# A fused adaLN, convolution and RWKV-7 block on one core: the first phase's instruction order on all engines and transfers, traced as tasks

## The chip, the core and the metric

The kernel runs on one core of one Trainium2 chip. A core has a matrix engine (TensorE, PE in the profile; its weight loads are PEld), VectorE (DVE), ScalarE (ACT), GpSimd (POOL) and SyncE (SP), which here issues the DMA transfers. Each engine works through its own list of instructions in order; an instruction that waits for a semaphore holds up all that stand behind it on that engine. The metric is device microseconds of one execution of the whole program. Numbers are float32; products that need float32 accuracy at speed are made from a high and a low part of each operand (type float32r).

## The reference

What is computed, for 2048 tokens of 1024 channels:

```python
def reference(x, c, ...):
    mod = silu(c) @ ada_w + ada_b
    shift, scale, gate = split(mod, 3)
    h = rmsnorm(x, norm_g) * (1 + scale) + shift
    p = h @ w_in                                   # 1024 -> 9344 columns
    c_val, c_gate, c_og, ts, r_og, g_conv, g_rwkv = split(p)
    # branch A: gated depthwise causal convolution of width 31, LayerNorm over channels
    u = depthwise_conv(c_val * sigmoid(c_gate)) + conv_b
    y_conv = (silu(layernorm(u)) * silu(c_og)) @ w_conv_out
    # branch B: RWKV-7, 16 heads of 64
    r, k, v, w_low, a_low = split(ts + mu * (shifted(ts) - ts))
    decay = exp(-exp(-softplus(-(w0 + tanh(w_low) @ w2)) - 0.5))
    a = sigmoid(a0 + a_low @ a2)
    kk = normalised(k * k_k);  k = k * (1 + (a - 1) * k_a)
    for t: state = state * decay_t - (state kk_t) (kk_t a_t)^T + v_t k_t^T;  o_t = state r_t
    y_rwkv = ((groupnorm(o) + sum(r k r_k) v) * silu(r_og)) @ w_rwkv_out
    m = sigmoid(g_conv) * y_conv + sigmoid(g_rwkv) * y_rwkv
    return rmsnorm(x + gate * (m @ w_out), final_g)
```

## The kernel before

**Tiling.** Tokens go in four blocks of 512 (`NB`, `TB`). Activations are held channel-major: 128 channels on the partitions, 512 tokens in a row. A projection tile is 128 output channels x 512 tokens; it takes 8 slices of the 1024 input channels, and each slice three float32r matmuls (high x high, high x low, low x high): 24 matmuls into one PSUM bank (`mm3k`, `mm3`, L172 to L185, with the matmul on L179). Two such banks alternate (`pm`, tag `main`). There are 73 projection tiles in a block.

**First phase.** A block first makes the LoRA tile (`lora_split`, L953) and then runs four slots (`slot`, L1039). A slot has 18 projection tiles: k, r and v for two pairs of heads, two convolution channels tiles (gate and value each), and eight gate tiles. `FILL` sets the order in which the twelve others go between the k, r and v tiles. The first-phase matmuls of a block are 73 x 24 = 1752, and 7008 in all.

Beside the projections run:

- `pair` (L501): decays, normalised keys and the products k by r of one pair of heads, with small matmuls on the PSUM tag `aux`. Its masked products are written on L590 and scaled on L597 into `As`.
- `group` (L645): for the four heads of a slot. It inverts unit triangular matrices: `As` goes to memory in 16 small DMAs (`dA`), comes back as `La`, 31 steps of two GpSimd operations build the inverse `TT` (L671, L673), it goes out as `dT` and comes back into `As` in 16 small DMAs (L684); VectorE transposes (L705), and TensorE makes the off-diagonal part (`lower`, L718, and `upper`, L722). Then comes the recurrence over 8 chunks of 64 tokens. A round of it is a chain of three links: state by KR (L775), VectorE's Xz (L780), As by Xz (L784), VectorE's uv (L795), tk by uv (L800), VectorE's new state S (L804). At the end the group is normalised (L822 to L831), transposed back (L839), gated and stored in `z_d`.
- `taps` (L878): the depthwise convolution, 31 VectorE operations on 512 tokens for each channel tile (L890).
- `lnorm_first` (L905): the LayerNorm of the block before, read back from memory; `xnorm` (L354): the RMSNorm of the next block; `gate_col`, `presplit`: columns and split weights for later.

**What sets the order.** Only TensorE's order is written by hand (`manual_schedule(engines={PE})`, L1084). The side work is a set of generators. `mm3` advances a clock by `US_K` = 0.684 us for each three matmuls (`tick`), and a generator yields a pair (its own TensorE time, a delay after which it goes on) or a condition. For instance, a group waits 35 + 25 us behind its inverse and 2.6, 2.5 and 3.3 us between the links of a round. The other engines and the DMA queue are ordered by the framework's scheduler, which takes `high_priority(HP)` and, for the taps, a low priority (`-LOWP`) into account.

**Buffers.** `hx` is a ring of seven 128 x 512 tiles for the side work (`HXB`), `w` one of six for weights (`WB`), `t2` one of two for evacuations. Weights of the input projection are split into high and low part in block 0, stored, and loaded split in blocks 1 to 3 (`load_w`, L149).

**Second phase.** `rproj` and `cproj` of block 0 run with the last group's recurrence still under way (L1146 to L1149); then the output projection of each block, with the two branch projections of the next.

Of the kernel before, what the change touches and what calls it, by code (L numbers as in the profile page):

```python
# [9 lines left out]
F32 = mybir.dt.float32  # L10
# [8 lines left out]
P = 128  # L19
# [14 lines left out]
W2 = 4  # L34
# [12 lines left out]
US_MM, US_K = 0.228, 0.684  # L47
LOWP = 1500
# [18 lines left out]
def hybrid_block(ctx: ExitStack, tc: tile.TileContext, x, vecs, convk, w2a2, final_g, ada, w_in, w_co, w_ro, w_o, crow, out,  # L67
                 seq=2048, groups=(0, 1, 2, 3), phase2=True, dbg=None):
    nc = tc.nc
    NB = seq // TB  # L70
    dbg = dbg or {}
# [20 lines left out]
    make_identity(nc, ident)  # L92
# [11 lines left out]

    def rsqrt(y, x_, pool, eng, t=None):
        if t is None:
            t = pool.tile(list(x_.shape), F32, name="rs_t", tag="rs_t")
        eng.tensor_scalar(out=y.bitcast(I32), in0=x_.bitcast(I32), scalar1=-0.5, scalar2=float(0x5F3759DF),
                          op0=ALU.mult, op1=ALU.add)
        for _ in range(3):  # L110
            eng.tensor_tensor(out=t, in0=y, in1=y, op=ALU.mult)
            eng.scalar_tensor_tensor(out=t, in0=t, scalar=-0.5, in1=x_, op0=ALU.mult, op1=ALU.mult)
            eng.scalar_tensor_tensor(out=y, in0=t, scalar=1.5, in1=y, op0=ALU.add, op1=ALU.mult)
# [9 lines left out]
    lo_dve = [False]  # L123
# [7 lines left out]
    def presplit(name, n, half):  # L131

        i = f"{n[0]}_{n[1]}" if name == "o" else n
        back = kept.setdefault((name, n), [dp.tile([P, KT, P], F32R, name=f"k{p_}_{name}{i}", tag=f"k{p_}_{name}{i}")
                                           for p_ in "hl"])
        hs = slice(half * 4, half * 4 + 4)
        st, hi, lo = hx("w_st"), hx("w_hi"), hx("w_lo")
        nc.sync.dma_start(st.rearrange("p (k n) -> p k n", k=4), wsrc[name][n][:, hs, :])
        if name == "o":
            gr = hx("w_gr")  # L140
            nc.sync.dma_start(gr[:, :256], grow_d[n[0] * 256:n[0] * 256 + 256].unsqueeze(0).broadcast_to([P, 256]))
            s4 = st.rearrange("p (k n) -> p k n", n=256)
            nc.gpsimd.tensor_tensor(out=s4, in0=s4, in1=gr[:, :256].unsqueeze(1).broadcast_to([P, 2, 256]), op=ALU.mult)
        nc.scalar.copy(hi.bitcast(F32R), st)
        nc.gpsimd.tensor_tensor(out=lo.bitcast(F32R), in0=st, in1=hi, op=ALU.subtract)
        for d_, s_ in zip(back, (hi, lo)):
            nc.sync.dma_start(d_[:, hs, :].bitcast(F32), s_.rearrange("p (k n) -> p k n", k=4))

    def load_w(name, n, hl=None):  # L149
# [11 lines left out]
        with tc.high_priority(HP):  # L161
            nc.scalar.copy(hi, st)  # L162
            lo_eng = nc.vector if lo_dve[0] or (name != "in" and wcount[0] % 4 < W2) else nc.gpsimd
# [17 lines left out]

    def mm3(ps, w, a):
        for k in range(KT):
            mm3k(ps, w, a, k)
            tick(US_K)  # L185
# [34 lines left out]

    now, tasks = [0.0], []

    class Task:

        def __init__(self, gen):
            self.gen, self.at, self.cond, self.done = gen, now[0], None, False
            tasks.append(self)

        def ready(self):
            return self.at <= now[0] and (self.cond is None or self.cond())  # L230

        def step(self):
            try:
                r = next(self.gen)
            except StopIteration:
                self.done = True
                tasks.remove(self)
                return
            if callable(r):
                self.cond = r  # L240
            else:
                self.cond = None
                now[0] += r[0]
                self.at = now[0] + r[1]

    def poll():
        moved = True
        while moved:
            moved = False
            for t in list(tasks):  # L250
                if not t.done and t.ready():
                    t.step()
                    moved = True

    def tick(us):
        now[0] += us
        poll()

    def drain(*ts):
        poll()  # L260
        while not all(t.done for t in ts):
            at = [t.at for t in tasks if t.at > now[0] and (t.cond is None or t.cond())]
            assert at, "no task can go on"
            now[0] = min(at)
            poll()
# [80 lines left out]
    closed = [None]  # L346

    def hx(name):
        return xp.tile([P, TB], F32, name=name, tag="hx")

    def spare(name):
        return closed[0](name) if closed[0] else hx(name)

    def xnorm(b, tts):  # L354
        if not tts:
            return
        held = []
        for tt in tts:
            t0 = b * TB + tt * P
            ss = e2.tile([P, 8], F32, name="ss")  # L360
            xh = []
            for half in range(2):
                xt = hx("xt")
                nc.sync.dma_start(xt, x[t0:t0 + P, half * TB:half * TB + TB])
                xh.append(xt)
            for half in range(2):
                nc.scalar.activation(hx("xsq"), xh[half], AF.Square, accum_out=ss[:, half:half + 1])
            vs, rs = ss[:, 2:3], ss[:, 3:4]
            with tc.high_priority(HP):
                nc.vector.tensor_tensor(out=vs, in0=ss[:, 0:1], in1=ss[:, 1:2], op=ALU.add)  # L370
                nc.vector.tensor_scalar(out=vs, in0=vs, scalar1=1.0 / D, scalar2=RMS_EPS, op0=ALU.mult, op1=ALU.add)
                rsqrt(rs, vs, e2, nc.vector, ss[:, 4:5])
                for kh in range(2):
# [944 lines left out]
```

## Time and profile before

| | |
|---|---|
| median of 3 runs | 3033.8 us (3033.46 to 3036.6) |
| the profiled execution's own time | 3034.01 us |
| its span, first to last instruction | 3032.2 us |
| mean granted TensorE clock | 0.969 |
| projection matmuls of the first phase (L179, 3 x 2304) | 970.6 + 918.6 + 915.4 us busy |
| convolution taps (L890) | 928 x 0.751 us on DVE |
| inverse on POOL (L671, L673) | 179.8 + 191.3 us |

How to read it: the page is one execution on the chip. A line of the groups of instructions gives source line, engine, operation, output and inputs, shapes and count, then the busy time in us and the mean of one in ns, and then the engine's idle time ahead of them with what ended it. Start-up lasts to about 65 us, the first phase to about 2434 us. TensorE matmuls are pipelined, so neighbours overlap and a busy TensorE is not a TensorE at its peak. Idle time of an engine that is not the bottleneck costs nothing by itself.

### The profile page before, as it was taken

How to read it: one execution, taken by the hardware profiler on the slowest of the kernel's cores; microseconds unless marked ns; L12 is line 12 of the kernel's file. 1: busy time of each engine (PE TensorE's matmuls, PEld its weight loads, DVE VectorE, ACT ScalarE, POOL GpSimd, SP SyncE). 2: the span in 40 equal slices, each digit the busy share in tenths (PEclk: the TensorE clock that was granted, in tenths of full speed). 3: DMA queues.
4: the chain of work that ended last, by engine and by line, in shares of the span. 5: the costliest groups of instructions: out<-in, count | busy, mean ns of one | idle time of the engine just before them, and what ended most of it. 6: DMA issues, size and time to landing. Idle time of an engine off the chain costs nothing. (4 is left out here: it accounts for less than half of the span.)

```text
span 3032.2 us, 51026 instructions
## 1 busy us (share of the span) xinstructions
PE 2817.1 (93%) x18640; PEld 2297.6 (76%) x18640; DVE 2072.0 (68%) x4160; ACT 1001.3 (33%) x1936; POOL 1229.8 (41%) x1790
## 2 busy tenths in 40 slices
PE   6889798999799999999999999999999999899998
PEld 5767686777687777777878777778787778788988
DVE  6867777779676778676767777666778755753433
ACT  4424343434233324242423242323323323421211
POOL 3464637352536355425373655253644500400000
PEclk9989899999899999999999999999999999999999
DMA  8677657686757666857676668565656666976665
GB/s 309 234 247 249 217 204 257 204 268 197 241 187 258 198 203 218 284 173 240 191 257 203 210 217 305 168 208 171 193 184 213 237 210 195 336 250 222 215 222 174
DMA packets 363146, 680.00 MB, mean 224 GB/s; under 512 B 135632, under 2 KB 154384, under 8 KB 362896
## 3 DMA queue, kind: packets, MB, share of 16 engines
q1 hardware_dynamic: 362896, 676.75, 67.0%
q8 instruction: 147, 2.41, 0.3%
q14 instruction: 103, 0.84, 0.1%
HBM read 494.08 MB, written 181.41 MB: 223 GB/s over the span
## 5 line engine op out<-in xcount | busy, mean ns | idle before, releaser
L179 PE MATMUL ps_main<-h_hi,w_hi 128*128 128x512 f32 x2304 | 970.6, 421 | 19.7 <-DMA w_hi<-kh_in 15.1
L179 PE MATMUL ps_main<-h_hi,w_lo 128*128 128x512 f32 x2304 | 918.6, 399 | 7.2 <-POOL w_lo L164 4.0
L179 PE MATMUL ps_main<-h_lo,w_hi 128*128 128x512 f32 x2304 | 915.4, 397 | 1.3 <-DVE h_lo L397 1.1
L890 DVE SCALAR_TENSOR_TENSOR acc<-u,ck,acc 128x512 f32<-128x512 f32 x928 | 696.7, 751 | 15.9
L179 PEld LDWEIGHTS ps_main<-h_hi,w_hi 128*128 128x128 f32 x2304 | 442.9, 192 | 115.5 <-issue 9.9
L179 PEld LDWEIGHTS ps_main<-h_hi,w_lo 128*128 128x128 f32 x2304 | 440.7, 191 | 114.4 <-POOL w_lo L164 6.2
L179 PEld LDWEIGHTS ps_main<-h_lo,w_hi 128*128 128x128 f32 x2304 | 443.6, 193 | 81.6 <-DVE h_lo L397 2.9
L804 DVE SCALAR_TENSOR_TENSOR S<-xo,pe,Se 64x64 f32<-64x64 f32 x512 | 144.5, 282 | 140.1 <-PE xo L800 130.5
L671 POOL TENSOR_TENSOR itmp<-La,TT 128x126 f32<-128x126 f32 (+22 forms) x496 | 179.8, 363 | 130.2 <-DMA La<-dA 85.2
L162 ACT CAST w_hi<-w_st 128x1024 fp32r<-128x1024 f32 x103 | 108.1, 1049 | 301.4 <-DMA w_st<-w_co_t 124.8
L673 POOL TENSOR_TENSOR TT<-TT,itmp 128x126 f32<-128x126 f32 (+22 forms) x496 | 191.3, 386 | 36.8
L164 POOL TENSOR_TENSOR w_lo<-w_st,w_hi 128x1024 fp32r<-128x1024 f32 x50 | 120.4, 2408 | 131.2 <-ACT w_hi L162 67.3
L779 ACT ACTIVATE Se<-S,pe 128x128 f32<-128x128 f32 x256 | 88.9, 394 | 169.5 <-DVE S L804 169.4
L164 DVE TENSOR_TENSOR w_lo<-w_st,w_hi 128x1024 fp32r<-128x1024 f32 x53 | 65.6, 1238 | 97.2 <-PE ps_main L179 54.8
L795 DVE TENSOR_TENSOR uv<-xo,rn 64x256 f32<-64x256 f32 x128 | 53.6, 419 | 111.4 <-PE xo L784 99.3
L784 PEld LDWEIGHTS xo<-Xz,As 128*64 128x64 f32 x1024 | 70.0, 138 | 68.8 <-DVE Xz L780 32.0
L753 ACT COPY Xz<-xo 64x256 f32<-64x256 f32 x128 | 47.0, 367 | 211.9 <-PE xo L758 141.7
L780 DVE TENSOR_TENSOR Xz<-xo,Xz 64x256 f32<-64x256 f32 x128 | 53.5, 418 | 86.0 <-PE xo L775 78.9
L845 POOL TENSOR_TENSOR oc<-oc,zt 128x512 f32<-128x512 f32 x64 | 81.7, 1285 | 66.6 <-ACT oc L841 39.6
L784 PE MATMUL xo<-Xz,As 128*64 128x64 f32 x1024 | 87.9, 230 | 20.9 <-DVE Xz L780 20.8
L590 DVE TENSOR_TENSOR As<-aux,maskA 128x512 f32<-128x512 f32 x128 | 83.0, 682 | 30.9 <-PE aux L587 30.4
L587 PE MATMUL aux<-KR,BK 64*128 64x128 f32 x1024 | 82.2, 291 | 17.8 <-DVE As L590 9.3
(299 smaller groups left out, 5493.7 us busy)
## 6 DMA issues: line engine op xcount, KB each, us to landing
w_hi<-kh_in SPq DMA_DIRECT2D x219, 512.0 KB, 4.2
w_lo<-kl_in SPq DMA_DIRECT2D x219, 512.0 KB, 5.3
w_st<-w_in_t SPq DMA_DIRECT2D x73, 512.0 KB, 4.5
kh_in<-w_hi SPq DMA_DIRECT2D x71, 512.0 KB, 2.9
kl_in<-w_lo SPq DMA_DIRECT2D x71, 512.0 KB, 3.6
lny<-y_d SPq DMA_DIRECT2D x72, 256.0 KB, 4.4
w_hi<-kh_ro SPq DMA_DIRECT2D x32, 512.0 KB, 3.9
w_lo<-kl_ro SPq DMA_DIRECT2D x32, 512.0 KB, 5.3
```

The costliest lines, as they stand in the source:

```text
L162: nc.scalar.copy(hi, st)
L164: lo_eng.tensor_tensor(out=lo, in0=st, in1=hi.bitcast(F32), op=ALU.subtract)
L179: nc.tensor.matmul(ps[:, qs], ww[:, k, :], aa[k][:, qs], start=(k == 0 and t == 0 and q == 0), stop=(k == KT - 1 and t == 2 and q == ms - ...
L587: nc.tensor.matmul(pA[hh][:, c // 2, es], BK[hs, cc, es], KR[hs, cc, es], start=(c == 0), stop=(c == 3), skip_group_check=True)
L590: nc.vector.tensor_tensor(out=Asb[:, hh, c4 * 4:c4 * 4 + 4, :].rearrange("p (a e) n -> p a (e n)", e=2), in0=pA[hh], in1=flat(maskA).unsqu ...
L671: nc.gpsimd.tensor_tensor(out=tmp[:, :ni, :nt], in0=La[:, j:j + 1, j + 1:].broadcast_to([P, ni, nt]), in1=TT[:, :ni, j:j + 1].broadcast_to ...
L673: nc.gpsimd.tensor_tensor(out=TT[:, :ni, j + 1:], in0=TT[:, :ni, j + 1:], in1=tmp[:, :ni, :nt], op=ALU.add)
L779: nc.scalar.mul(Se[:, q, :], Sg[:, q, :], R[q]["pe"][:, c:c + 1])
L784: nc.tensor.matmul(b_[pr_, q, hs], As[q][:, hh, c, kcol(e)], Xz[:, e, q, hs], start=(n == 0), stop=(n == 3), skip_group_check=True)
L804: nc.vector.scalar_tensor_tensor(out=Sg[hs, q, hs], in0=b_[hs, 2 + q, hs], scalar=R[q]["pe"][hs, c:c + 1], in1=Se[hs, q, hs], op0=ALU.mult ...
L845: nc.gpsimd.tensor_tensor(out=oc, in0=oc, in1=zt, op=op)
L890: nc.vector.scalar_tensor_tensor(out=acc if i + 1 < HALO else yj, in0=u[:, i:i + TB], scalar=ck[:, j, i:i + 1], in1=acc, op0=ALU.mult, op1 ...
```

## The change

The first phase is now traced by hand for all five engines and for the DMA issues (`manual_schedule()` without a list): the program order on each engine is the order in which the Python code runs. Which step runs next is decided by a clock kept while tracing. Every instruction goes through a wrapper (`Lane`), so that in a profile of the changed kernel all of them carry the wrapper's line.

- `note` keeps, for every engine and for the DMA, the time until which it is busy (`vt`), for every tile when it is written and last used (`ready`, `used`), and for every pool tag the buffers in use. Costs are constants: `RATE`, `DMA_RATE`, `SEM`, `SWITCH`. TensorE's time is `now`.
- A `Task` has a rank. `poll` runs the first task in rank order whose condition has come: pieces of data are ready (`ok`), an engine's backlog is below a number (`idle`), a PSUM bank is free (`bank`), a ring has room (`Ring.room`), or a flag is set (`when`). Groups and evacuations have rank 0, weight loads 1, pairs 2, side work 3, taps 4. `until` moves the clock on when TensorE has nothing that it may do.
- `group`, `pair`, `taps`, `lnorm_first`, `xnorm`, `gate_col`, `presplit`, `lora_split` and the evacuations are rewritten with such conditions in place of delays, and take tiles from rings and give them back. The evacuation of a projection tile is a task of its own (`evac`); `project` waits until that of the tile before the last is done.
- Weights are loaded two or three tiles ahead (`plan`, `Load`). The split of the next block's input is fed into the last projection of a block (`hstep`), where it stood at the start of the next.
- `slot` starts when the group two slots back is normalised. Five fill tiles instead of two (`FIRST`) stand between the pairs, and the last slot has an order of its own (`LAST`).
- `rproj` and `cproj` of block 0 become tasks as well (`early_rows`, `lsteps`), and `W2` now decides on which engine a weight's low part is made.

```diff
-US_MM, US_K = 0.228, 0.684
-LOWP = 1500
+LAST = ("c", "1", "c", "3", "4", "2", "1", "3", "4", "2")
+DMA_RATE = 330e3
+FIRST = 5
+AHEAD = 0.7
+BANKS = {"aux": 2, "late": 1, "xo": 2}
+SEM, SWITCH = 0.1, 0.1
+RATE = {"DVE": (0.16, 1.08e-3), "ACT": (0.20, 0.8e-3), "POOL": (0.12, 2.2e-3)}
...
+    def note(name, op, out, ins):
+        k_ = key(out)
+        t = max([now[0], vt.get(name, 0.0), used.get(k_, 0.0)] + [ready.get(key(a), 0.0) + SEM for a in ins])
...
+        elif name == "SP":
+            vt["SP"] = t + 0.07
+            vt["DMA"] = max(vt["DMA"], t) + size(out) * out.shape[0] * 4 / DMA_RATE
+            end = vt["DMA"] + 1.9
+        else:
+            c0, c1_ = RATE[name]
+            end = vt[name] = t + c0 + c1_ * max([size(out)] + [size(a) for a in ins[:1]])
...
+    def until(pred):
+        poll()
+        while not pred():
+            ws = [w for w in (t.when() for t in tasks) if w is not None and w > now[0]]
+            now[0] = min(ws)
+            poll()
...
     def mm3(ps, w, a):
         for k in range(KT):
+            until(lambda: len(a[1]) > k)
             mm3k(ps, w, a, k)
-            tick(US_K)
+            if khook[0]:
+                khook[0](k)
+            poll()
...
+    def project(a, src):
+        ahead()
+        w = loads.pop(0)
+        ahead()
+        until(lambda: w.here)
+        drain(*evacs[-2:-1])
+        ps = pm.tile([P, TB], F32, name="ps_main", tag="main")
+        mm3(ps, w.hl, a)
+        Task(w.drop(), 1)
+        return ps
...
     def group(G, before):
-        yield lambda: G.tri == 2
+        yield when(lambda: G.tri == 2)
+        yield ok(*As)
...
+        yield ok(La, TT)
         for j in range(31):
+            yield idle("POOL", 0.5)
...
-        lo_dve[0] = True
-        yield 0.0, 35.0
-        lo_dve[0] = False
-        yield 0.0, 25.0
-        yield lambda: G.pairs == 2 and (before is None or before.done)
+                yield idle("SP", 0.1)
+        yield when(lambda: G.pairs == 2 and (before is None or before.chained))
+        yield ok(*As)
...
-            yield 0.6, 2.6
+            yield ok(Xz)
...
-            yield 1.1, 2.5
+            yield ok(uv)
...
-            yield 0.6, 3.3
+            yield ok(Sg)
...
     def taps(b, j, u, before):
...
         for i in range(HALO):
-            if i % 2:
-                yield 0.0, 2.0
+            yield idle("DVE", AHEAD)
...
     def lnorm_first(b):
...
         for j in range(KT):
+            yield hx.room(3, 1)
+            yj, ct, th = yload(j), hx.take("lnc"), hx.take("lnth")
+            nc.sync.dma_start(ct, co_dram[b][j])
+            yield ok(yj, rl)
             nc.gpsimd.tensor_tensor(out=yj, in0=yj, in1=mean, op=ALU.subtract)
+            yield idle("POOL", 0.3)
             nc.gpsimd.tensor_tensor(out=yj, in0=yj, in1=rl, op=ALU.mult)
...
+    def lora_split(ps, out_):
+        yield hx.room(3)
+        lf, ll, lx = hx.take("lora"), hx.take("lora_lo"), hx.take("lora_x")
...
+    def slot(b, g, h, lora, new):
+        until(lambda: not Gs[:-1] or Gs[-2].normed)
+        G = opened(b, g, h, lora)
+        groups_.append(Task(group(G, Gs[-1] if Gs else None), 0))
...
-    with tc.manual_schedule(engines={mybir.EngineType.PE}):
+    with tc.manual_schedule():
...
-        drain(*pairs_, *convs)
+        drain(*pairs_, *convs, *side, *evacs, *groups_[:-1])
```

More of the change, by code (lines that the diff above doesn't have):

```diff
@@ L33 @@
 HP = 3000
-W2 = 4
+W2 = 0.3
 HB = 8
@@ L218, in xload0 @@
         return xs
[L221 to L265, printed above, removed]
     late, early = ExitStack(), ExitStack()
```

782 lines of the change are left out of this document (544 added, 238 removed).

## The prediction

> **What bounds the kernel now.** The page comes first: its span, busy shares and clock row.
>
> ```profile
> span 3032.2 us, 51026 instructions
> ...
> PE 2817.1 (93%) x18640; PEld 2297.6 (76%) x18640; DVE 2072.0 (68%) x4160; ACT 1001.3 (33%) x1936; POOL 1229.8 (41%) x1790
> ...
> PEclk9989899999899999999999999999999999999999
> ...
> PE 16%; DVE 4%; DMA 2%; POOL 1%; issue 1%; SPq 0%; ACT 0%; DVEq 0%; POOLq 0%; ACTq 0%
> ```
>
> TensorE (PE) sets the time, also in the chain of waits (last line), where it has the largest share. The next view is busy time by stage: start-up, first phase, the stretch in which the last recurrence runs beside block 0's output projections, and the rest.
>
> ```profile
> core 0: us, PE busy (x) PEld busy (x) DVE busy (x) ACT busy (x) POOL busy (x), PEclk, DMA share, GB/s
> ...
> 65.00:2434.00 2369.00, 2210.86 (x15004) 1773.56 (x15003) 1739.45 (x3512) 819.02 (x1572) 1160.60 (x1731) 0.97 0.67 221
> 2434.00:2663.00 229.00, 210.94 (x1369) 177.11 (x1368) 138.68 (x244) 76.64 (x150) 48.08 (x32) 0.96 0.73 250
> ```
>
> In the first phase TensorE is idle for 2369 - 2211 = 158 us, and a granted clock of 0.97 costs about 0.03 x 2369 = 71 us. So 229 us is all that a better order can win there. The second stretch holds 18 us more. Where the idle time goes is in the list of TensorE's waits up to 2434 us:
>
> ```profile
> engine line waited for: us in total, times, longest us
> PE late L839 <- POOL uv L831: 23.3, 4, 16.1
> PE xo L784 <- DVE Xz L780: 20.8, 14, 3.8
> ...
> PE ps_main L179 <- DMA w_hi<-kh_in: 15.1, 3, 5.8
> PE late L839 <- ACT oc L841: 13.4, 14, 1.1
> PE aux L587 <- DVE As L590: 9.3, 7, 4.5
> PE late L722 <- DVE Qs L728: 9.1, 8, 1.9
> PE late L718 <- DVE T L705: 7.9, 2, 4.6
> ...
> PE xo L758 <- DVE S L804: 7.5, 3, 4.4
> ...
> PE ps_main L179 <- ACT w_hi L162: 4.3, 1, 4.3
> PE ps_main L179 <- POOL w_lo L164: 4.0, 4, 1.5
> ...
> PE ps_main L179 <- DVE w_lo L164: 2.0, 1, 2.0
> ```
>
> No single wait rules. About a third belongs to transposes and weights that the fixed delays placed too early, and the rest to short handoffs with VectorE (DVE).
>
> **The part of the change that speaks against it: the triangular inverse.** Each of the 16 groups needs one: mask on VectorE (L590, L597), DMA out (dA) and in (La), 62 GpSimd steps (L671, L673), DMA out (dT) and in (As), eight transposes (L705), and then TensorE's `lower` (L718). The last group, and the one before the last block boundary, show how long that takes:
>
> ```profile
> 2381.48 1.61 DVE L597 TENSOR_TENSOR As<-As,rn 64x512 f32<-64x512 f32 x2
> ...
> 2389.26 1.13 SPq L662 DMA_DIRECT2D La<-dA  x2
> ...
> 2423.16 1.34 SPq L677 DMA_DIRECT2D dT<-TT  x2
> ...
> 2426.97 9.19 SPq L684 DMA_DIRECT2D As<-dT  x16
> ...
> 2435.91 1.94 DVE L705 STREAM_TRANSPOSE T<-As 32x128 f32<-32x128 f32 x8
> ...
> 1801.15 3.41 DVE L597 TENSOR_TENSOR As<-As,rn 64x512 f32<-64x512 f32 x2
> ...
> 1872.40 0.30 DVE L705 STREAM_TRANSPOSE T<-As 32x128 f32<-32x128 f32 x1
> ```
>
> From the end of L597 to the last transpose it takes 2437.85 - 2383.09 = 54.8 us in the one and 1872.70 - 1804.56 = 68.1 us in the other; I take the middle, 61.4. What TensorE does meanwhile is mostly projection matmuls, and their pace under this load is in the busy time of that tile:
>
> ```profile
> 2383.00:2456.00 73.00, 59.82 (x234) 44.88 (x234) 3.41 (x5) 4.79 (x8) 0.93 0.79 264
> ```
>
> 73 / 234 = 0.312 us for each, other matmuls and waits included. In the old TensorE order each group has 216 to 279 projection matmuls between its last L587 matmul and its `lower`, so the inverse is covered. In the new order twelve groups have 180 to 321. Four have far fewer: group 8 of 16 has 96, group 12 has 84, group 15 has 108, group 16 has 93. There `lower` stands in TensorE's queue, and everything behind it waits.
>
> The code says why. At the boundary into blocks 2 and 3 the LoRA product's evacuation waits for three `hx` buffers. The layer norm of the block before holds them, and its GpSimd work goes ahead only when GpSimd's backlog is under 0.3 us, behind the inverse (rank 0, backlog under 0.5 us). The third product may not be traced until that evacuation is done, so the inverse's remaining GpSimd steps, its DMAs and `lower` all land before it. Group 15 meets the rule that a slot opens only when the group two before it is normalised; group 16 meets the `drain` at the end of the phase.
>
> Price of a place: 61.4 us less its matmuls at 0.312. That is 31.5, 35.2, 27.7 and 32.4 us, in sum 126.8. At group 15 another 3.67 rounds of the recurrence stand with no projection between them. What VectorE does in a round is in the groups of instructions:
>
> ```profile
> L890 DVE SCALAR_TENSOR_TENSOR acc<-u,ck,acc 128x512 f32<-128x512 f32 x928 | 696.7, 751 | 15.9
> ...
> L804 DVE SCALAR_TENSOR_TENSOR S<-xo,pe,Se 64x64 f32<-64x64 f32 x512 | 144.5, 282 | 140.1 <-PE xo L800 130.5
> ...
> L795 DVE TENSOR_TENSOR uv<-xo,rn 64x256 f32<-64x256 f32 x128 | 53.6, 419 | 111.4 <-PE xo L784 99.3 <-PE xo L749 10.8
> L780 DVE TENSOR_TENSOR Xz<-xo,Xz 64x256 f32<-64x256 f32 x128 | 53.5, 418 | 86.0 <-PE xo L775 78.9 <-ACT uv L625 5.8
> ```
>
> 0.418 + 0.419 + 4 x 0.282 = 1.97 us, and with one convolution tap in front of each link, as the new order has it, 3 x 0.751 more: 3.67 x 4.2 = 15 us (7 without taps). **Sum: +142 us**; from 4 x 54.8 - 118.9 + 7 = 107 to 4 x 68.1 - 118.9 + 15 = 169, where 118.9 is the 381 matmuls at 0.312.
>
> **What it removes.** The transposes that waited for ScalarE's oc (13.4 here, 5.2 in smaller rows) now wait in the tracing for a free bank, and products go between. Weight waits (15.1 + 4.3 + 4.0 and 3.1 in smaller rows) go, since loads are traced as soon as a ring has room and the next block's split is fed into the last product. Half of the 23.3 us behind uv goes: two of the new slot starts still have that transpose right behind GpSimd work. Together 18.6 + 26.5 + 11.6 = 57 us. Their share of the clock loss is 57 / 158 x 71 = 26 us; four long stalls bring some of it back:
>
> ```profile
> 336.10:353.20 17.10, 4.39 (x14) 3.51 (x15) 9.96 (x22) 4.92 (x7) 7.59 (x7) 0.50 0.64 223
> ...
> 162.00:165.40 3.40, 3.40 (x10) 2.61 (x9) 2.48 (x4) 1.03 (x1) 2.85 (x8) 0.50 0.90 328
> ```
>
> After the 16.1 us gap, 4.39 us of matmuls ran at half clock and lost 2.2 us, so four stalls cost 9. **Sum: -57 - 26 + 9 = -74 us**; bounds: nothing to the whole 229.
>
> By the Trainium skill (TensorE: Matmul & The Clock Gate, "HAM oscillation — how this bites in real kernels") only idle gaps over about 3.4 us cost clock, which would leave most of the 26 us unwon and the sum some 15 us higher. Here the trace disagrees: the second row is at half clock and follows the wait of 2.0 us for w_lo, the last in the list of waits above.
>
> **What it moves without a sure sign.** In the recurrence a round had 33 to 39 projection matmuls between its links, and now has mostly 15 (3, 6, 6). Three are 0.77 us of TensorE's busy time (59.82 / 234 each), in which VectorE must do L780 (0.418), leaving 0.35 us for two handoffs and for a tap that is under way (0.751). A short wait at each of the 384 links costs, at 0.3 us, up to 115 us; the 28 us of L780 and L804 in the list of waits can go at best. I take no change. The clock of the new tracing is too fast in places. It charges 0.71 us for any 512-wide VectorE operation, 0.23 us for a scan of 64, and 0.07 us for a DMA issue:
>
> ```profile
> L524 DVE TENSOR_TENSOR_SCAN M<-one,M 128x64 f32<-128x64 f32 x256 | 90.9, 420 | 8.4 <-ACT M L516 8.1
> ...
> L572 DVE SCALAR_TENSOR_TENSOR rk<-r,hrk,ta 128x512 f32<-128x512 f32 x32 | 43.3, 1352 | 0.3
> ...
> L705 DVE STREAM_TRANSPOSE T<-As 32x128 f32<-32x128 f32 x128 | 31.0, 277 | 9.5 <-DMA As<-dT 8.2
> ...
> L684 SPq DMA_DIRECT2D As<-dT x256: 302/430/1596, 189.1 to 2435.7; - x128
> ```
>
> VectorE has slack over the phase (1739 of 2369 us), so this shows as lateness, not as load. Sixteen small DMAs take 6.9 us against 1.1 modelled, twice a group, so La and As land 11.6 us later than the order assumes. GpSimd's first step and VectorE's transposes then wait at the head of their queues, with weight splits, evacuations and the links of the recurrence behind them. Two PSUM banks cover two products, 48 matmuls or 15 us at the pace above, so I charge nothing to the twelve ordinary groups; without that cover it is up to 12 x 11.6 = 139 us. Choosing VectorE or GpSimd for a weight's low part (W2) and the evacuations as tasks lie beside TensorE's work and are charged nothing; uncovered they would wait on the same banks.
>
> **After the phase.** The last recurrence ends after 111 projection matmuls of the second phase, not 381, so its norm and transposes leave the end of the 229 us stretch. Of the 18 us idle there I take 12 off, bounds 0 and 18.
>
> **Sum.** 142 - 74 - 12 = +56 us. The profiled execution took 3034.0 us by its own time (span 3032.2), the median of the runs is 3033.8: **3090 us**.
>
> **Rivals.**
> 1. *Readiness pays more than four stalls cost.* The new order breaks even when it wins 142 - 12 = 130 of the 229 us. For it: most waits are handoffs that a readiness test is made for, and the idle clock follows them. Against: the links get tighter, and its constants are low for the operations above. If three quarters go (-172), the stalls stay near 120 and 15 come off behind the phase: -67, **2967 us**.
> 2. *Late semaphores.* The head-of-queue waits for La and As are not covered by the PSUM banks: 8 us in each of twelve groups is 96 on top of +56, **3186 us**. It decides as soon as As lands after its transposes' turn; against it, today's transposes (L705 above) wait 8.2 us in all for that DMA.
> 3. *The order hardly matters*, because TensorE is full and stalls trade places: within 0.2% (6 us, about what runs of this kernel can tell apart), **3034 us**.
>
> **How the numbers follow.** The forecast has 0.42 with its own range 3045 to 3135, rival 1 0.36, rival 2 0.17, rival 3 0.05. Rival 1 lies some 55 us either side of its figure, rival 2 about as far, so 2955 to 3190 leaves out a little under 2 in 10. Faster 0.37, same 0.06, slower 0.57.
>
> **What would show it.** Right: four TensorE gaps of 20 us or more, at `lower` or right ahead of it, near 51%, 76%, 94% and 100% of the first phase's projection matmuls, with GpSimd in its inverse steps or SP issuing As; the waits for oc and for weights nearly gone; short waits at L780's consumer more frequent. Wrong: no such gaps, or a granted clock of 0.99 in the phase. If VectorE's idle time behind As is large in every group, rival 2 was right.

## The result and the profile after

| | before | after |
|---|---|---|
| median of the runs beside each other, us | 3033.6 (3029.5 to 3036.6, 4 runs) | 3251.0 (3250.0 to 3252.3, 4 runs) |
| ratio after / before | | 1.072, 95% interval 1.0704 to 1.0735 |
| span of the profiled execution, us | 3032.2 | 3249.3 |

The changed kernel is 217 us slower. The prediction had the sign, with 56 us. These are the lines of the page of the changed kernel that answer to those of before (span, busy shares, granted clock in 40 slices, chain of waits by engine), and the mean granted clock:

```profile
span 3249.3 us, 51086 instructions
...
PE 2869.5 (88%) x18640; PEld 2324.2 (72%) x18640; DVE 2153.6 (66%) x4153; ACT 997.1 (31%) x1936; POOL 1270.6 (39%) x1797
...
PEclk9999999999899999799989997999998969999999
...
PE 27%; DVE 7%; POOL 6%; DMA 5%; issue 2%; SPq 2%; ACT 1%; DVEq 0%; POOLq 0%; ACTq 0%
```

```profile
core 0: 3249.3 us, clock 0.938
```

The 217 us split in two. TensorE's idle time went from 3032.2 - 2817.1 = 215.1 to 3249.3 - 2869.5 = 379.8 us: +165. Its busy time went up by 52.4 us with the same 18640 matmuls; they ran slower, and the mean granted clock fell from 0.969 to 0.938. The clock records of the two traces account for nearly all of it: TensorE was busy at half clock for 141 us before and for 243 us after, and half of the difference is 51 us. Where the idle time is, the list of TensorE's waits of the changed kernel says (us in total, times, longest):

```profile
PE late L126 <- DVE T L126: 134.3, 13, 34.8
PE ps_main L126 <- ACT h_hi L126: 18.8, 3, 8.5
PE ps_main L126 <- ACT w_hi L126: 18.3, 5, 5.6
PE late L126 <- POOL uv L126: 18.0, 5, 7.3
...
PE aux L126 <- POOL KR L126: 16.4, 13, 3.2
PE ps_main L126 <- DMA w_hi<-kh_in: 16.1, 5, 4.7
PE aux L126 <- ACT wl L126: 13.0, 5, 6.0
PE xo L126 <- DVE Xz L126: 10.8, 18, 1.8
...
PE ps_main L126 <- POOL w_lo L126: 8.9, 5, 3.2
...
PE xo L126 <- DVE S L126: 3.6, 5, 1.1
...
PE late L126 <- ACT oc L126: 1.7, 2, 0.9
```

The first line is `lower` behind VectorE's transposes: 134.3 us, where before it was 7.9 us on the PSUM tag `late` and 2.9 on `aux`, so +123.5. Four waits make up 108.7 of it, in groups 8, 12, 15 and 16 (first matmul of `lower`, the idle time ahead of it in brackets):

```profile
1340.31 0.23 PE L126 MATMUL late<-T,As 32*32 32x32 f32 x1 [31.78 <-DVE T L126]
...
1988.33 0.23 PE L126 MATMUL late<-T,As 32*32 32x32 f32 x1 [34.77 <-DVE T L126]
...
2431.19 0.26 PE L126 MATMUL late<-T,As 32*32 32x32 f32 x1 [12.31 <-DVE T L126]
...
2626.55 0.26 PE L126 MATMUL late<-T,As 32*32 32x32 f32 x1 [29.86 <-DVE T L126]
```

All other idle time is +41 us, of which 31 lie in the first phase, for which the prediction had -57. The waits for oc are nearly gone, those for weights are not, and waits for h_hi and wl are new. Two stretches of the changed kernel's timeline show where new ones arise (start, duration, queue, instruction):

```profile
644.41 8.37 SPq L126 DMA_DIRECT2D dA<-As  x16
...
657.24 0.43 SPq L126 DMA_DIRECT2D hf<-xT  x1
...
663.59 0.80 PE L126 MATMUL ps_main<-h_hi,w_hi 128*128 128x512 f32 x1 [8.51 <-ACT h_hi L126]
...
885.62 9.85 SPq L126 DMA_DIRECT2D As<-dT  x16
...
895.52 0.43 SPq L126 DMA_DIRECT2D wf<-w2a  x1
...
898.08 0.79 PE L126 MATMUL aux<-lw,wl 128*128 128x512 f32 x1 [5.95 <-ACT wl L126]
```

The issues of the inverse's sixteen small DMAs occupy SP for 8.37 and 9.85 us. One of them takes 0.43 us in the median, 6.9 us for sixteen; most of the rest is SP's own waits between them. The traced clock charges 0.07 for one, 1.1 us for sixteen. The load of the next block's input (hf) and of the decay weights (wf), a few places further back on SP, come that much later, and with them a cast on ScalarE and a product. Last, the busy time by stage, cut at the last projection of the first phase and at the first output product (the second is how long block 0's two products and the last recurrence take), before and then after:

```profile
65.00:2435.00 2370.00, 2211.86 (x15009) 1774.22 (x15007) 1739.45 (x3512) 819.35 (x1573) 1160.60 (x1731) 0.97 0.67 221
2435.00:2556.00 121.00, 113.59 (x766) 90.91 (x766) 64.04 (x122) 33.28 (x63) 5.02 (x4) 0.96 0.59 195
```

```profile
65.00:2597.00 2532.00, 2248.99 (x15012) 1792.56 (x15012) 1823.09 (x3519) 815.89 (x1571) 1179.05 (x1705) 0.94 0.62 206
2597.00:2780.00 183.00, 131.64 (x782) 100.65 (x782) 92.26 (x150) 51.13 (x94) 64.29 (x66) 0.80 0.53 182
```

The phase takes 162 us more, the stretch behind it 62 more (29.9 of them the stall of group 16); the rest of the second phase gives 7 back.

### The profile page after: what moved, and what is told of

The parts are those of the page before. It is cut to its first block, busy times and chain, and to the rows that moved or that the text cites. A ratio compares the mean times of both kernels' runs of the same rounds, so it can differ in the third digit from the quotient of the medians.

```text
span 3249.3 us, 51086 instructions
## 1 busy us (share of the span) xinstructions
PE 2869.5 (88%) x18640; PEld 2324.2 (72%) x18640; DVE 2153.6 (66%) x4153; ACT 997.1 (31%) x1936; POOL 1270.6 (39%) x1797
## 4 chain that ended last, share of the span: by engine, by line
PE 27%; DVE 7%; POOL 6%; DMA 5%; issue 2%; SPq 2%; ACT 1%; DVEq 0%; POOLq 0%; ACTq 0%
PE ps_main L126 17%; PE pout L126 5%; PE xo L126 4%; SPq L126 2%; POOL TT L126 1%; POOL itmp L126 1%; DVE acc L126 1%; PE aux L126 1%; DVE S L126 1%; PE late L126 1%; POOL lny L126 1%; DMA out<-xt 1%; DVE y L126 0%; DMA w_lo<-kl_in 0%; DMA dA<-As 0%
## 5 line engine op out<-in xcount | busy, mean ns | idle before, releaser
L126 PE MATMUL ps_main<-h_hi,w_hi 128*128 128x512 f32 x2304 | 986.6, 428 | 60.0 <-ACT h_hi L126 18.8
L126 PE MATMUL ps_main<-h_hi,w_lo 128*128 128x512 f32 x2304 | 929.5, 403 | 12.3 <-POOL w_lo L126 6.6
L126 POOL TENSOR_TENSOR w_lo<-w_st,w_hi 128x1024 fp32r<-128x1024 f32 (+1 forms) x89 | 181.2, 2035 | 317.1 <-ACT w_hi L126 283.5
L126 POOL TENSOR_TENSOR itmp<-La,TT 128x126 f32<-128x126 f32 (+22 forms) x496 | 195.7, 395 | 145.5 <-DMA La<-dA 114.5
L126 ACT CAST w_hi<-w_st 128x1024 fp32r<-128x1024 f32 (+1 forms) x135 | 127.3, 943 | 251.8 <-DMA w_st<-w_co_t 126.6
L126 ACT ACTIVATE th<-ps_main 128x512 f32<-128x512 f32 x160 | 95.4, 596 | 319.2 <-PE ps_main L126 272.9
L126 POOL TENSOR_TENSOR lny<-lny 128x512 f32<-128x512 f32 x90 | 117.6, 1313 | 125.4 <-DMA lny<-y_d 116.2
L126 PE MATMUL xo<-uv,As 128*64 128x64 f32 x2048 | 156.9, 230 | 1.5 <-issue 0.9
L126 PEld LDWEIGHTS xo<-uv,As 128*64 128x64 f32 x2048 | 135.2, 141 | 14.2 <-DVE S L126 6.9
L126 PE MATMUL late<-T,As 32*32 32x32 f32 x512 | 25.6, 215 | 134.3 <-DVE T L126 134.3
L126 PEld LDWEIGHTS late<-T,As 32*32 32x32 f32 x512 | 23.4, 131 | 141.1 <-DVE T L126 72.4
```

The source lines that it names most:

```text
L126: r = f(*a, **k)
```

## The experiments

Each is the changed kernel (3251.0 us) with the edit shown, timed beside the kernel before (medians 3030.5 to 3034.9 us in the four groups of runs).

| run | us | ratio to before, 95% interval |
|---|---|---|
| 1 the wait at four `lower` taken away | 3236.9 | 1.0658 (1.0633 to 1.0684) |
| 2 layer norm's step at 0.7 us of backlog | 3202.1 | 1.0551 (1.0530 to 1.0572) |
| 3 traced order on TensorE alone | 3376.2 | 1.1125 (1.1106 to 1.1145) |
| 4 an SP issue charged 0.45 us | 3151.7 | 1.0382 (1.0363 to 1.0400) |
| 5 last group's `lower` held back | 3236.6 | 1.0670 (1.0652 to 1.0689) |
| 6 six constants | 3014.7 | 0.9932 (0.9908 to 0.9955) |
| 7 six constants, other values | 2998.1 | 0.9884 (0.9869 to 0.9900) |
| 8 as 7, SP issue at 0.07 | 3077.3 | 1.0149 (1.0125 to 1.0173) |
| 9 as 7, second pair after 5 fills | 3062.5 | 1.0082 (1.0057 to 1.0108) |
| 10 as 7, queues free after the phase | 2985.4 | 0.9843 (0.9813 to 0.9873) |
| 11 second pair after 2 fills | 3254.5 | 1.0741 (1.0717 to 1.0765) |
| 12 as 11, SP issue at 0.45 | 3213.7 | 1.0607 (1.0580 to 1.0634) |

### 1. Is a stall the wait of `lower` for the inverse?

```diff
+    CUT = (7, 11, 14, 15)
...
-            ENT[TRE].tensor_tensor(out=tri, in0=tri, in1=rq[sl].rearrange("p c h -> p h c").unsqueeze(3).broadcast_to(
+            ENT[TRE].tensor_tensor(out=tri, in0=tri, in1=(zer if CUT is None or 4 * b + G.g in CUT else rq)[sl].rearrange("p c h -> p h c").unsqueeze(3).broadcast_to(
...
-                        nc.sync.dma_start(As[q][sl, hh, e::2, sl], dT[:, q, hh, :, e, bk, :])
+                        if CUT is None or 4 * b + g in CUT:
+                            tc.nc.sync.dma_start(spill[sl, hh], dT[:, q, hh, :, e, bk, :])
+                            note("SP", "dma_start", As[q][sl, hh, e::2, sl], [dT])
+                        else:
+                            nc.sync.dma_start(As[q][sl, hh, e::2, sl], dT[:, q, hh, :, e, bk, :])
```

> The changed kernel with every instruction in its place, but in groups 8, 12, 15 and 16 the sixteen transfers of the inverse land in a spare tile and not in As, and the triangle of As is multiplied by zeros (the output is wrong there). So `lower` has nothing to wait for in these four groups, while GpSimd, SP and the transfers do all their work. Stall theory (the four waits are their own price): the four TensorE gaps, 31.8 + 34.8 + 12.3 + 29.9 = 109 us, go, and 5 to 15 us of half clock behind them: 3127 to 3137 us, still some 100 over the kernel before. Rival (in a stall the other engines catch up, so that without it their lateness shows elsewhere): half of it returns as other waits, 3180 to 3200 us. Second rival (all of the loss hangs on the stalls): near 3034 us.

Measured: 3236.9 us, 14 less. No theory had so little: most of the four gaps stayed, and in the same places (27.2, 29.1, 10.1 and 22.0 us, 88 of 109). The waits of this run:

```profile
PE late L126 <- DVE T L126: 59.8, 9, 22.0
PE late L126 <- ACT la L126: 56.4, 2, 29.1
```

Its timeline at group 8 shows why:

```profile
1327.49 0.24 POOL L126 TENSOR_TENSOR TT<-TT,itmp 128x16 f32<-128x16 f32 x1
1327.69 1.26 POOL L126 TENSOR_TENSOR lny<-lny,lnr 128x512 f32<-128x512 f32 x1
...
1328.98 0.81 ACT L126 ACTIVATE lnth<-lny,hlb,hlg 128x512 f32<-128x512 f32 x1 [20.77 <-POOL lny L126]
...
1330.67 0.69 DVE L126 SCALAR_TENSOR_TENSOR lny<-lnth,lny 128x512 f32<-128x512 f32 x1 [16.23 <-ACT lny L126]
...
1332.84 1.76 DVE L126 STREAM_TRANSPOSE T<-As 32x128 f32<-32x128 f32 x8
...
1334.74 0.23 PE L126 MATMUL late<-T,As 32*32 32x32 f32 x1 [27.22 <-ACT la L126]
```

The transposes need nothing from the inverse any more. But in VectorE's queue they stand behind a layer norm step, that one waits for ScalarE's, that one for GpSimd's, and GpSimd's stands behind the last step of the inverse. All queues run in traced order, so all of them meet at the point where the traced clock ran ahead without a product for TensorE. (ScalarE's la, which the list names, ended 0.07 us after the last transpose, so that the two waits end together; la stands behind the same layer norm step, by way of lora on VectorE.) Taking away one wait of this knot gave back only the 2 to 8 us by which it was the last.

### 2. The place in the tracing that makes two of the stalls

```diff
             yield ok(yj, rl)
             nc.gpsimd.tensor_tensor(out=yj, in0=yj, in1=mean, op=ALU.subtract)
-            yield idle("POOL", 0.3)
+            yield idle("POOL", 0.7)
             nc.gpsimd.tensor_tensor(out=yj, in0=yj, in1=rl, op=ALU.mult)
```

> One constant: the layer norm's GpSimd step may be traced with GpSimd 0.7 us behind, not 0.3. By the traced order this gives `lower` 222 and 213 projection matmuls of cover in groups 8 and 12 where the changed kernel has 96 and 84, and 120 and 141 in groups 15 and 16 where it has 108 and 93. Stall theory: the gaps of 31.8 and 34.8 us go, 60 matmuls at 0.312 us take 19 us off the other two, and about 5 us of half clock go with them: 3155 to 3165 us. Rival (the layer norm's steps now stand between the inverse's on GpSimd and make it later): one gap of 10 to 20 us stays at each of the two boundaries, 3180 to 3200 us. If hx was not the cause: 3251 us.

Measured: 3202.1 us, 49 less; more time than the stall theory's 3155 to 3165, and just beyond the rival's range, though not by its mechanism:

```profile
PE late L126 <- DVE T L126: 43.2, 11, 10.5
PE aux L126 <- ACT wl L126: 38.6, 9, 7.9
...
PE ps_main L126 <- ACT o_hi L126: 16.7, 2, 16.3
```

The waits at `lower` fell from 134.3 to 43.2 us and none is over 10.5; in groups 8 and 12 they are 2.1 and 2.6 us. So the boundary stalls did come from the layer norm's step; that it acts by holding the `hx` ring is read from the code. But wl rose from 13.0 to 38.6, o_hi from 2.8 to 16.7, and DVE mr from 4.8 to 15.6. We read this as late loads and casts that the stalls had covered; no run separates it. Groups 15 and 16, with 120 and 141 matmuls of cover, waited 10.5 and 5.7 us, where 61.4 us less their matmuls at 0.312 gives 24.0 and 17.4.

### 3. Do the fixed orders of the other four queues cost by themselves?

```diff
-    with tc.manual_schedule():
+    with tc.manual_schedule(engines={mybir.EngineType.PE}):
```

> TensorE keeps the traced order; the orders of VectorE, ScalarE, GpSimd and SP are left to the scheduler, as in the kernel before. Queue theory (the rest of the loss, some 90 us beside the stalls, comes from the other four queues keeping the traced order, in which a small transfer or a cast stands behind sixteen DMA issues): the waits for h_hi (18.8), wl (13.0), w_hi (18.3) and KR (16.4) mostly go, the four gaps at `lower` stay near 109: 3180 to 3200 us. Rival (it is TensorE's order alone): within 10 us of 3251. Second rival (the scheduler's own order does not fit this TensorE order): 3270 us or more.

Measured: 3376.2 us. In time the queue theory and the first rival fall, and the second rival holds. `lower` alone now waits 193.7 us on the tag `late`, the longest 55.9:

```profile
PE late L126 <- DVE T L126: 193.7, 9, 55.9
```

The scheduler's order brings the inverse later than this TensorE order needs it. But one part of the queue theory's forecast did come: the waits for h_hi, wl, wlo, KR and the projections' weights, 34.3 us before the change and 99.2 in the changed kernel, are 22.8 us here (h_hi 4.4, w_hi 7.6, w_lo 10.8, none for the others). So these belong to the traced order of the other four queues, as far as the longer stalls did not cover them.

### 4. The charge for a DMA issue

```diff
-            vt["SP"] = t + 0.07
+            vt["SP"] = t + 0.45
```

> One constant of the traced clock: an issue on SP is charged 0.45 us (the trace shows 0.32 to 0.6), not 0.07. The order changes everywhere: `lower` is short of cover in groups 6, 10, 14 and 16 (81, 114, 102 and 165 matmuls against 197 needed), the other twelve have 201 or more. Stall theory: 36 + 26 + 30 + 10 = 102 us of gaps in place of 124, and no bare recurrence at group 15: 3200 to 3220 us. Queue theory adds that waits behind bursts of issues (h_hi, wl, part of w_hi) fall by 30 to 40 us with their clock: 3160 to 3180 us. If both fail it stays at 3240 us or more.

Measured: 3151.7 us, 99 less, more than either theory gave. Around groups 6, 10 and 14, short of cover, TensorE does stall, but ahead of their `lower`, at the last transposes of groups 5, 9 and 13, for which the next slot waits:

```profile
964.44 0.69 PE L126 MATMUL late<-ident,uv 128*128 128x128 f32 x2 [17.66 <-POOL uv L126]
...
2219.84 0.69 PE L126 MATMUL late<-ident,uv 128*128 128x128 f32 x2 [14.63 <-POOL uv L126]
```

The one between them is 18.96 us; that is 51 us where 36, 26 and 30 were expected. `lower` itself waits 11.7 us on `late`, where the changed kernel has 134.3; this, less what came at uv, is most of the 99 us. The waits that the queue theory named fell little: h_hi 18.8 to 14.7, wl 13.0 to 9.8, w_hi behind ScalarE 18.3 to 13.4 and behind the DMA 16.1 to 10.4, KR 16.4 to 14.4. With wlo and w_lo they are 82.8 us, 16 less, not 30 to 40.

### 5. The last group

```diff
+    closed = [None]
...
-        yield when(lambda: G.pairs == 2 and (before is None or before.chained))
+        yield when(lambda: G.pairs == 2 and (before is None or before.chained) and (
+            4 * b + g < 15 or closed[0] is not None and now[0] >= closed[0] + 15.0))
...
+        closed[0] = now[0]
         early.close()
```

> Only the last group's inverse is followed later: its transposes and `lower` may be traced from 15 us (by the traced clock) after the end of the first phase, so that projection rows of block 0 stand ahead of `lower` (129 matmuls of cover, not 93). If the stall at group 16 is `lower` traced too early, its gap (29.9 us) falls by the 36 matmuls, 11 us, and the recurrence ends later but still beside the second phase: 3235 to 3240 us. Rival (the first rows are not ready either, their loads start only when the phase is closed and their splits stand in the same queues): the gap only changes its name, from VectorE's T to ScalarE's o_hi: 3251 us.

Measured: 3236.6 us, 14 less. The time is in the first range, but that is luck: the trace speaks for the rival. The wait for o_hi is 32.7 us in one piece, and `lower` waits 109.2 in all, 25 less. The first rows of block 0 are as late as the inverse, and the gap changed its name. TensorE's idle time is the same in all (380.0 us, 379.8 in the changed kernel); what fell is its busy time, from 2869.5 to 2858.6 us, with less of it at half clock.

### 6 and 7. The constants of the clock and of the ranks

Run 6 (in run 7 AHEAD is 0.4, the scans' backlog 1.0, and the layer norm of the block before starts in slot 1, not 2):

```diff
-W2 = 0.3
+W2 = 0.0
...
-FIRST = 5
-AHEAD = 0.7
+FIRST = 2
+AHEAD = 0.5
...
-            vt["SP"] = t + 0.07
+            vt["SP"] = t + 0.45
...
-                yield idle("DVE", 0.3)
+                yield idle("DVE", 2.0)
...
-            yield idle("POOL", 0.3)
+            yield idle("POOL", 0.7)
```

> Six constants of the tracing and nothing else: an SP issue charged 0.45 us, the layer norm's GpSimd step allowed 0.7 us of backlog, the scans 2.0 us of VectorE backlog, taps 0.5 us ahead in place of 0.7, the second pair of a group after 2 fills in place of 5, and a low part on VectorE as soon as GpSimd is the later. By the traced order every group has 231 to 318 projection matmuls between its last L587 matmul and `lower`. Clock theory (readiness tracing is sound, its clock and its ranks misplaced the inverse and with it all five queues): no gap over 6 us at `lower` or at the transposes of uv in the phase, half-clock time near that of before (193 us), 3030 to 3070 us. Rival (five queues in a fixed order cost by themselves: waits for weights, wl, h_hi and KR and the clock behind them stay as they are): 3090 to 3120 us.

> As the run before it, but taps 0.4 us ahead, scans 1.0 us, and the layer norm of the block before starts one slot earlier. Same cover (222 to 339 matmuls). Both theories expect it within 10 us of that run; more than 20 us between them would mean that the place of single tasks still decides, not the cover of the inverse.

Measured: 3014.7 and 2998.1 us, both under every range given, and 0.7 and 1.2% faster than the kernel before. The clock theory's signs came nearly as stated: in run 6 the longest wait at `lower` is 6.8 us, and half clock took 198 us. Of the rival's waits those for weights did stay (47.1 us in the changed kernel, 51.1 and 46.4 here), while h_hi and wl went from 31.8 to 8.1 and 4.6. Of run 7, the page, the wait at `lower`, the mean clock and the busy time by stage:

```profile
span 2997.8 us, 51087 instructions
...
PE 2810.1 (94%) x18640; PEld 2288.6 (76%) x18640; DVE 2128.6 (71%) x4158; ACT 998.6 (33%) x1936; POOL 1244.8 (42%) x1792
```

```profile
PE late L126 <- DVE T L126: 16.4, 5, 9.0
```

```profile
core 0: 2997.8 us, clock 0.970
```

```profile
65.00:2363.00 2298.00, 2187.16 (x15011) 1756.43 (x15012) 1788.02 (x3515) 818.66 (x1573) 1168.26 (x1739) 0.98 0.68 227
2363.00:2532.00 169.00, 135.45 (x782) 102.47 (x781) 97.98 (x152) 49.88 (x92) 49.28 (x27) 0.82 0.58 194
```

The phase is 72 us shorter than before the change (2298 against 2370), with 111 us idle where it had 158, and the clock is back. The stretch behind it keeps 48 of the 62 us that the change added. The two runs lie 17 us apart with the same cover, more than the 10 expected and less than the 20 that would have spoken for single places; this stays undecided.

### 8, 9, 11 and 12. One constant at a time

Run 8 sets the SP charge of run 7 back to 0.07, run 9 its FIRST back to 5; run 11 is the changed kernel with FIRST at 2, run 12 the same with the charge of 0.45.

> The second retimed kernel with one constant set back: an SP issue is charged 0.07 us again. The cover of the inverse stays (189 to 285 matmuls in every group). If the charge for SP is what the retiming needs (bursts of sixteen issues stand ahead of loads that the order counts on), waits for weights, wl and h_hi come back by 30 to 60 us and the clock with them: 3050 to 3090 us. If the cover of the inverse alone decides: 2990 to 3015 us.

> The second retimed kernel with one constant set back: the second pair of a group starts after 5 fills again, not 2. Cover falls to 144 and 129 matmuls in groups 14 and 16, to 183 in group 4, and the slots wait longer for the group two before. If the place of the second pair sets when the inverse can start and so what stalls, two gaps of 15 to 20 us and longer waits behind uv come back: 3050 to 3080 us. If not: within 10 us of 2998.

> The changed kernel with one part of the change undone: the second pair of a group follows after 2 fills, as before the change, not after 5. Cover of the inverse by the traced order: group 15 gets 213 matmuls (108), groups 8, 12 and 16 stay short with 102, 78 and 48. By the price of the stalls alone: group 15 gives back 12 us of gap and 9 us of bare recurrence, group 16 costs 14 more: 3240 to 3250 us. If the late second pair costs by itself in every group (64 us in the retimed kernel): 3185 to 3200 us.

> Both at once on the changed kernel: 2 fills, and an SP issue charged 0.45 us. Cover is short in group 8 (99) and group 16 (135) alone. If the two effects add (99 us for the charge, 64 for the second pair): 3085 to 3095 us. If the slots' wait for the group two before, which sets the price of a late second pair, is only reached with all six constants: 3130 to 3150 us.

Measured: setting back the charge costs 79 us, setting back FIRST 64. Both times lie in the range of the first of the two readings, but what waits is not what it named. In run 9 `lower` has no long stall (longest 6.3 us); one wait behind uv of 20.0 us came, weights wait 20 us longer (46.4 to 66.7), wl 17 and o_hi 12. In run 8 waits for weights, wl and h_hi rose by 16 us, not 30 to 60. There no group is more than 8 matmuls short of cover, and still `lower` waits in nearly every one:

```profile
PE late L126 <- DVE T L126: 56.2, 14, 11.7
```

That is the mechanism of the prediction's second rival, an inverse that lands later than traced, at about 4 us a group: VectorE's transposes waited 60.3 us for the DMA of As in run 8, 16.6 in run 7. Put on alone, the same constants act otherwise: FIRST at 2 changes next to nothing (3254.5, just above the stall theory's range), and together with the charge it is 62 us worse than the charge by itself; neither range for run 12 holds. Why is not shown; our reading is that with the boundary stalls still there each constant only moves them. Run 11 is a test of their price. By 61.4 - 0.312 n, groups 8, 12 and 16 with n = 102, 78 and 48 should wait 29.6, 37.1 and 46.4 us:

```profile
1329.98 0.23 PE L126 MATMUL late<-T,As 32*32 32x32 f32 x1 [28.91 <-DVE T L126]
...
1992.93 0.23 PE L126 MATMUL late<-T,As 32*32 32x32 f32 x1 [38.34 <-DVE T L126]
...
2631.53 0.25 PE L126 MATMUL late<-T,As 32*32 32x32 f32 x1 [44.27 <-DVE T L126]
```

They do, within 2.1 us. In run 12 the same formula gives 30.5 us for group 8 (99 matmuls) and 19.3 for group 16 (135); measured are 36.1 and 2.8 us.

### 10. The end of the phase

```diff
         early.close()
 
+    with tc.manual_schedule(engines={mybir.EngineType.PE}):
         ob = ctx.enter_context(tc.tile_pool(name="ob", bufs=2, side="right", reuse_waits="tile"))
```

> The second retimed kernel, but from the end of the first phase on only TensorE keeps the traced order; the other four queues are left to the scheduler for block 0's two products, as in the kernel before. In the retimed kernel TensorE is idle 34 us between the last product of the first phase and the first output product, against 7 before. If that is the price of traced queues across the border (loads and splits of block 0's rows stand behind the end of the first phase in every queue), 20 to 30 us return: 2970 to 2980 us. Rival (the last recurrence then competes with the scheduler's order): 3000 us or more.

Measured: 2985.4 us, 13 less than run 7, the right sign and half the size. The busy time by stage has the stretch behind the phase at 153 us, from 169:

```profile
2362.00:2515.00 153.00, 125.11 (x780) 97.14 (x780) 106.42 (x160) 49.12 (x90) 49.79 (x27) 0.89 0.59 194
```

TensorE's idle time in it fell only from 34 to 28 us; the rest is matmuls at a higher clock (0.89, from 0.82). This is the fastest version found, 1.6% under the kernel before.

## Why the prediction was right about the stalls and wrong about the rest

**The triangular inverse (+142): right in place and in what the tracing does there, a little large.** The four gaps stood in the four groups named, 31.8, 34.8, 12.3 and 29.9 us against 31.5, 35.2, 27.7 and 32.4. The bare rounds of group 15 have waits of 0.4 to 1.5 us that add up to 9.3, where 15 were allowed. So 118 of 142; the missing part is nearly all group 15. Its inverse took 53.0 us (from the end of the last mask at 2378.2 to that of the last transpose at 2431.1), not 61.4, and the 102 projection matmuls in that time came with so many others that TensorE was busy for 40.5 us, 0.40 us for each, not 0.312. Run 11 confirms the price at three other covers. It does not hold everywhere: it is 13.5 and 11.7 us too high in groups 15 and 16 of run 2, 16.5 too high in group 16 of run 12, and 5.6 too low in group 8 of run 12. One thing was too simple: "`lower` stands in TensorE's queue, and everything behind it waits". By run 1 the stall is the meeting point of all five queues, of which TensorE's, with `lower`, is one.

**What it removes (-57): the step that failed.** Of its three parts, oc came (19.6 to 2.7 us over the whole run) and uv in part (23.3 to 18.0). "Weight waits go, since loads are traced as soon as a ring has room" did not: 26.5 us became 47.1 (w_hi and w_lo behind DMA, ScalarE, GpSimd and VectorE). And waits that the sum did not have came in: h_hi 18.8, wl and wlo 16.9, KR up by 8.6. Of the 47.1 us, 17.8 are behind loads and 29.3 behind the splits on ScalarE, GpSimd and VectorE, which the prediction's reason, earlier loads, does not reach. In the first phase idle time beside `lower` is +31 us; without the 9.3 of group 15's bare rounds, which the first term has, it is +22. So this term was off by 79 us.

The prediction had seen one source: "Sixteen small DMAs take 6.9 us against 1.1 modelled". It asked who waits for La and As, and what stands behind those waits on GpSimd and VectorE, found cover for them and charged nothing. It did not ask what else is queued behind sixteen issues on SP. Runs 4 and 8 show what the charge is worth with the rest of the order that follows from it, -99 and 79 us, but most of that is `lower`, the uv transposes and the clock. That the new waits belong to the traced order of the four other queues, run 3 supports (99.2 us to 22.8); that SP's bursts alone cause them is not shown, and run 4, with the charge put right, speaks against it (82.8 us stay).

**The clock (-26 + 9): the sign was wrong.** It was derived from the idle time, and this grew. TensorE's busy time rose by 52.4 us, by the half clock behind more waits. In runs 7 and 10, with idle time at 188 and 180 us, it is 2810 and 2801 us and the clock 0.970 and 0.973: the clock follows the waits, as argued, only in the other direction. It does not follow their sum alone: run 9 has 240 us of idle time and is at 2810 us too.

**After the phase (-12): wrong.** The stretch grew by 62 us, 32 without the stall of group 16, which the first term has. The prediction moved the last recurrence but not the loads of block 0's rows, which, by the code, now stand behind the drain of the phase on every queue. Run 5 (the gap renamed to o_hi) and run 10 (13 us back with free queues) support this; a part of it stays unexplained.

**The moved work charged at nothing.** The tight links of the recurrence cost nothing, as taken: waits for Xz went from 20.8 to 10.8 us, for S (both consumers) from 10.6 to 3.6. The ordinary groups: 134.3 - 108.7 = 25.6 us at their `lower`, so the second rival's price (96) was not reached. Its sign, VectorE's idle time behind As, did come in part: 53.1 us, 1.6 to 7.1 us in each of 14 groups, where the kernel before had 8.2 in all.

```profile
DVE T L126 <- DMA As<-dT: 53.1, 35, 3.9
```

With the charge at 0.45 it is 14.2 us in run 4. So the inverse did land later than traced, and most of that lateness was covered, as the prediction took it; run 8 shows it uncovered. Five fills ahead of the second pair were not priced at all; alone that is nothing (run 11), in the retimed kernel it is 64 us.

**The rivals.** The sign of the forecast came out because the stalls were priced about right; its size did not, since three other terms went the wrong way. Readiness did not pay in this kernel, but it can: the same machinery with other constants came to 2998 and 2985 us, the latter 18 over the first rival's figure. The ledger of the changed kernel: +123.5 at `lower`, +41 other idle time, +52 slower matmuls, in sum 217. Not settled: which of the other constants of run 7 are needed, how the 41 us split between SP's bursts and other causes, and why run 12 is slower than run 4.

## What to carry to other kernels

An order traced by a clock hangs on the clock's constants (one of them was worth 79 and 99 us here): compare every charge with the profile's mean for that operation, first the ones that come in bursts, and look behind the burst on the same queue, not only at its result. Where tracing can move its clock on without giving the bounding engine work, count the work that stands between a long chain's start and its consumer; the shortfall times the pace was a good price at the block boundaries, within 6 us each time, and up to 17 us too high elsewhere. Once all queues are in a fixed order, a stall need not have a single cause to cut, as run 1 shows: change the rule that placed it, and change constants together, since one alone may give little.

## What the hardware showed

- A DMA issue takes SP 0.43 us in the median, for the inverse's small DMAs as for the single loads beside them (rows above, and L684 of the kernel before: 302 to 1596 ns, median 430). The Trainium skill (DMA: Bandwidth & Descriptors, "Anatomy of one DMA — SWDGE (gpsimd) path") has about 50 ns of sequencer dispatch, for DMAs that GpSimd issues, which no run here has; these rows, for SP, are eight to nine times that.
- Half clock can follow a short wait. A wait of 1.29 us, the only one over 0.15 us in the 15 us before, and 3.4 us at half clock that begin 1.8 us after it; and the 10 us behind the stall of 31.78 us, in which 8.45 us of matmuls ran at half clock:

```profile
1263.62 0.57 PE L126 MATMUL aux<-bones,sq 128*64 128x2 f32 x14 [1.29 <-ACT sq L126]
```

```profile
1265.50:1268.90 3.40, 3.40 (x10) 2.62 (x9) 3.30 (x4) 0.83 (x2) 2.63 (x3) 0.51 0.19 69
1340.70:1350.70 10.00, 8.45 (x138) 6.91 (x134) 3.75 (x8) 1.23 (x2) 2.55 (x2) 0.50 0.31 80
```

  By the Trainium skill (TensorE: Matmul & The Clock Gate, "HAM oscillation — how this bites in real kernels") the rule is that no idle gap should be over about 3.4 us. The second row agrees; the first shows that a shorter gap can cost clock too. Most do not: of 91 waits under 1.2 us in this trace, 23 have half clock in the 3.5 us behind them, of 35 waits of 2.5 us and more, 33.
